# Down-weight differences in attention, kept split halves, and a rearranged block end in a decoder step on one core

## The chip, the cores and the metric

The kernel runs on one core of a Trainium2 chip. The metric is the device time of one execution in microseconds (us), as the median of several runs. Profiles are of one profiled execution.

The engines are named as in the profile: PE (TensorE, matmuls), PEld (its weight loads), DVE (VectorE), ACT (ScalarE), POOL (GpSimd) and SP (SyncE, which here only issues DMA transfers).

## The reference

One layer of a decoder is computed for 2048 prompt rows and for 8 × 4 sample rows that have a cache of 2048 keys and values. `h` stands for the rows of either group.

```python
q, k, v, u, g = split(rmsnorm(x, norm1_g) @ w_in)          # 1024 -> 5 x 512
att  = merge of 3 dilated-window attention branches (8 heads of 64)
gate = per chunk of 128 rows: tril(sgu_w) @ layernorm(g) + sgu_b
x = x + concat([att, u * gate]) @ w_out                    # 1024 -> 1024
h = rmsnorm(x, norm2_g)
x = x + (silu(h @ w_gate) * (h @ w_up)) @ w_down           # 1024 -> 2816 -> 1024
y = rmsnorm(x, final_g)
```

The outputs are `y` of both groups, the new keys and values, and the normalised `g` rows of the samples. The new caches of the samples are the old ones shifted by four rows, so 64 MB go from DRAM to DRAM.

## The kernel before

**Stages.** The times are those of the trace. The kernel first computes the projections, the spatial gate and the samples' attention (0 to 560 us). Then comes prompt attention (560 to about 900 us). The output projection and the feed-forward part (FFN) follow in three blocks of 6, 6 and 4 row tiles. The last block also holds the sample rows. The output projection and norm of block 0 end at 985 us. FFN block 0 runs to 1480, a block end to 1600, FFN block 1 to 2040, a block end to 2160, FFN block 2 to 2520, and the closing norm to 2557 us.

**Split products.** Each fp32 product is made of three matmuls: high × high, high × low and low × high. An operand is split by an ACT copy that rounds to the high half, and a subtraction on DVE or POOL that leaves the low half. `split_dw` does this for down weights (lines 1644 and 1645).

**The FFN.** The hidden width is cut into NF = 22 slices `f`. The up part of a slice is seven products, `product(B, u, q)` with q from 0 to 6, of a seven-product scheme in place of eight. Its operands are sums of weight parts that POOL and ACT prepare for later slices (lines 1579 and 1583). Two slices together make one group n (0 to 10) of seven down products, `down_product(B, k)`, k = 7n + p. Their left operands are sums of the hidden parts, made by `h_even` after the even slice and `h_odd` after the odd one; `high_of` and `lows_of` split them. Their right operands are w_down parts or differences of those. A down product issues nine matmuls for six tiles (line 1660) and three accumulations on DVE (line 1662).

**Down weights.** During the projections `down_rows` loads two row groups of w_down, `down_sums` makes four differences on POOL, and `down_keep` stores all seven parts in the DRAM buffer `dd_d`. In every block, `load_dw` fetches part k into one of two ring places after the product k − 2 was issued, and `split_dw` splits it two up products ahead of its use. POOL takes all low halves in block 1 and those of even k in blocks 0 and 2; DVE takes the others.

**What sets the order.** Each engine works through its instructions in the order in which they were issued. Through the projections and attention, a hand-made table sets that order: `at(step, phase, fn, ...)` puts a call at a step and a phase within it, and all is issued in that order. Attention begins at step B0 = 240. In the FFN the order is that of the loops: `one(u, q)` issues an up product and what belongs beside it, and `later(n, fn)` puts a call n ticks ahead, where each up product or down product at a block end is a tick. SP is a single in-order queue for nearly all transfers. `roll(n)` issues n pieces of 512 KB of the cache copies on it.

**The block end.** `next_block` is called after the last up product of a block. It issues the previous block's last eight down products with `h_odd` and the splits of `w_out` in between. After them `open_unit` starts the output projection of each tile of the next block (24 matmuls, lines 1407 to 1409), whose left operand `split_cat` has split (line 1399, the low half on DVE). `first_end`, `second_unit` and the norm follow.

## Time and profile before

| what | value |
|---|---|
| median of the runs (3 runs: 2557.12 to 2560.17 us) | 2557.52 us |
| the profiled execution's own time | 2560.03 us |
| its span, first to last instruction | 2557.5 us |
| mean granted TensorE clock | 0.980 |
| matrix work: PE busy | 2421.8 us, 95% of the span |
| instructions | 40544 |
| data moved by DMA | 512.36 MB, mean 200 GB/s |

The share of busy time is an average over stages that differ. So the windows of the stages, with the idle time of PE in each, tell more than the totals do. A row of the waits gives the engine, the tile and line that waited, what ended the wait, and then the total in us, the number of times and the longest. A row of the timeline gives start, length, engine, line and operation, output and input tiles with their shapes, and in brackets the engine's idle time ahead of it with what ended it. In a group the two numbers behind the bar are the busy time in us and the mean ns of one instruction.

### The profile page before, as it was taken

What the parts mean: (1) busy time and instruction counts of PE and PEld (TensorE: products, weight loads), DVE (VectorE), ACT (ScalarE), POOL (GpSimd) and SP (SyncE); (2) the same over time, 40 slices, a digit from 0 to 9 for tenths busy, and PEclk for the clock granted to TensorE, in tenths of its full rate; (3) what the DMA queues carried; (4) which work ended last, traced back from release to release, by engine and by line L of the source; (5) the groups of instructions that cost most, each with busy time, mean ns of one, the idle gap of its engine ahead of it and who ended that gap; (6) DMA issues with size and microseconds to landing.
All of it is one profiled execution on the core that took longest, in us unless ns stands there. A gap on an engine that the chain in (4) does not pass through costs nothing. (4 is left out here: it accounts for less than half of the span.)

```text
span 2557.5 us, 40544 instructions
## 1 busy us (share of the span) xinstructions
PE 2421.8 (95%) x13764; PEld 2080.4 (81%) x13764; DVE 1710.7 (67%) x3302; ACT 1242.6 (49%) x2773; POOL 1441.3 (56%) x1152
## 2 busy tenths in 40 slices
PE   8998998999999998999999989999999989999997
PEld 7876776657888778888988978999999967888886
DVE  4557564214777645778778786677767776888876
ACT  6323333224766646655655446443434346444444
POOL 2117463103777746777777734666666644666665
PEclk9999998999999999999999999999999999999999
DMA  9976877895456463655656562766665554666663
GB/s 290 281 235 226 273 239 237 281 297 201 146 183 197 108 199 110 200 185 181 192 176 205 173 189 98 233 202 199 199 202 192 189 184 134 212 204 216 217 214 113
DMA packets 326722, 512.36 MB, mean 200 GB/s; under 512 B 32535, under 2 KB 164808, under 8 KB 321396
## 3 DMA queue, kind: packets, MB, share of 16 engines
q1 hardware_dynamic: 319668, 497.72, 60.8%
q10 hardware_dynamic: 6848, 12.06, 1.7%
q8 instruction: 109, 1.79, 0.3%
q14 instruction: 97, 0.79, 0.1%
HBM read 401.77 MB, written 178.03 MB: 227 GB/s over the span
## 5 line engine op out<-in xcount | busy, mean ns | idle before, releaser
L1583 POOL TENSOR_TENSOR op<-fr,op 128x512 fp32r<-128x512 f32 x385 | 511.6, 1342 | 221.3 <-ACT op L1579 116.8
L1750 PE MATMUL ps_m<-xh,op 128*128 128x384 f32 (+3 forms) x1904 | 607.1, 319 | 1.9 <-DVE zn L1771 1.7
L1752 PE MATMUL ps_m<-xh,op 128*128 128x384 f32 (+3 forms) x1904 | 606.1, 318 | 0.0
L1751 PE MATMUL ps_m<-xl,op 128*128 128x384 f32 (+3 forms) x1904 | 605.7, 318 | 0.1
L1660 PE MATMUL ps_o<-hop 128*128 128x512 f32 x1260 | 343.4, 403 | 37.3 <-POOL hop L1645 26.5
L1750 PEld LDWEIGHTS ps_m<-xh,op 128*128 128x128 f32 x1904 | 361.5, 190 | 14.0 <-issue 1.9
L1751 PEld LDWEIGHTS ps_m<-xl,op 128*128 128x128 f32 x1904 | 361.0, 190 | 9.7 <-DVE xl L1496 0.4
L1752 PEld LDWEIGHTS ps_m<-xh,op 128*128 128x128 f32 x1904 | 360.8, 189 | 0.0
L1662 DVE TENSOR_TENSOR acc<-acc,ps_o 128x512 f32<-128x512 f32 x448 | 295.2, 682 | 26.9 <-PE ps_o L1660 20.6
L1660 PEld LDWEIGHTS ps_o<-hop 128*128 128x128 f32 x1260 | 230.6, 189 | 90.4 <-POOL hop L1645 38.7
L1645 POOL TENSOR_TENSOR hop<-hop 128x512 fp32r<-128x512 f32 x140 | 186.5, 1332 | 173.9 <-ACT hop L1644 158.6
L1579 ACT ACTIVATE op<-fr 128x512 fp32r<-128x512 f32 x396 | 238.7, 620 | 3.1 <-PE ps_m L1752 2.1
L1790 ACT ACTIVATE ps_t<-zn 128x384 f32<-128x384 f32 (+1 forms) x126 | 58.5, 464 | 365.4 <-DVE zn L1773 191.4
L320 PE MATMUL ps_s<-wh,xh 128*128 128x512 f32 x480 | 199.1, 415 | 6.3 <-ACT xh L137 5.9
L322 PE MATMUL ps_s<-wh,xl 128*128 128x512 f32 x480 | 190.8, 397 | 0.0
L321 PE MATMUL ps_s<-wl,xh 128*128 128x512 f32 x480 | 190.7, 397 | 0.0
L1644 ACT ACTIVATE hop<-hop 128x512 fp32r<-128x512 f32 x210 | 130.9, 623 | 56.6 <-DMA hop<-dd_d 54.7
L538 POOL TENSOR_TENSOR pr<-kv,qb 96x512 f32<-96x512 f32 x32 | 46.1, 1441 | 162.3 <-DMA kv<-in_cache_k_dram 75.6
L320 PEld LDWEIGHTS ps_s<-wh,xh 128*128 128x128 f32 x480 | 92.0, 192 | 49.2 <-issue 23.7
L1660 PE MATMUL ps_m<-hop 128*128 128x512 f32 x420 | 121.2, 397 | 0.0
L1583 POOL TENSOR_TENSOR op<-pair,op 128x512 fp32r<-128x512 f32 x63 | 86.9, 1382 | 50.9 <-ACT op L1579 50.8
L322 PEld LDWEIGHTS ps_s<-wh,xl 128*128 128x128 f32 x480 | 92.0, 192 | 20.8 <-DVE xl L140 0.2
(514 smaller groups left out, 5064.0 us busy)
## 6 DMA issues: line engine op xcount, KB each, us to landing
fr<-ab_d SPq DMA_DIRECT2D x308, 256.0 KB
hop<-dd_d SPq DMA_DIRECT2D x210, 256.0 KB
out_ks_dram<-in_cache_k_dram SPq DMA_DIRECT2D x56, 512.0 KB
out_vs_dram<-in_cache_v_dram SPq DMA_DIRECT2D x56, 512.0 KB
ab_d<-fr SPq DMA_DIRECT2D x88, 256.0 KB
qk_d<-pair SPq DMA_DIRECT2D x64, 256.0 KB
ab_d<-pair SPq DMA_DIRECT2D x63, 256.0 KB
kv<-in_cache_k_dram SPq DMA_DIRECT2D x64, 192.0 KB
```

The source lines that it names most:

```text
L320: pe.matmul(o[j], xh[:, k, :], wh, start=(k == 0), stop=False)
L321: pe.matmul(o[j], xh[:, k, :], wl, start=False, stop=False)
L322: pe.matmul(o[j], xl[:, k, :], wh, start=False, stop=(k == KD - 1))
L1579: act.activation(ops[f, j][0], ab[f][j], AF.Copy)
L1583: (pool if f or j in POOL_LOW else dve).tensor_sub(lo_, ab[f][j], hi.bitcast(F32))
L1644: act.activation(hi, lo_.bitcast(F32), AF.Copy)
L1645: (dve if k % 2 and (B.last or B.b0 == 0) else pool).tensor_sub(lo_, lo_.bitcast(F32), hi.bitcast(F32))
L1660: pe.matmul(ps, l_, r_, start=(new and y == 0), stop=(y == 2), skip_group_check=True)
L1662: dve.tensor_add(x[:, cs], x[:, cs], ps)
L1750: pe.matmul(out, wh[:, ks], xh[:, :, k], start=(k == 0), stop=False)
L1751: pe.matmul(out, wh[:, ks], xl[:, :, k], start=False, stop=False)
L1752: pe.matmul(out, wl[:, ks], xh[:, :, k], start=False, stop=(k == 3))
```

## The change

The change has five parts.

1. `down_rows`, `down_sums` and `down_keep` move from the projections to attention (steps 243 + 14n and on). Of the four differences of a group, two are made on POOL and two on DVE. The three parts that are plain pieces of w_down are copied from DRAM to DRAM during the projections (`down_plain`).
2. Block 1 stores both halves of each split down weight of groups 0 to 9 in a new DRAM buffer, `ds_d` (`keep_dw`). Block 2 loads both halves from there and splits nothing. In block 0 DVE makes all low halves; in block 1 POOL does, as before.
3. In blocks 0 and 2 the subtraction and low halves of `h_even` are made on POOL.
4. `roll` is called twice per slice in every block, where it was once, three times and twice.
5. At a block end the last down products stand in another order, with two `open_unit` calls among them. Six splits of `w_out` come ahead of the block end. The weights of the last group are loaded into free places of the operand buffers, which are allocated once for all blocks. `h_last` does in four parts what `h_odd` did in three. `split_cat` is spread over later ticks, and makes the low halves of all but the first two tiles on POOL.

The order of instructions in the program changes at three places, which are shown as engine, line, operation, output and input tiles. The line numbers of the two kernels differ by 1 to 16. The first place is POOL's order in the projections, beside a group's differences (`tu`, `tw`), the layer norm (`zn`) and the samples' scores (`pr`), before:

```order
L632 TENSOR_TENSOR tu<-tw 128x512
L629 TENSOR_TENSOR tw<-tw 128x512
L385 TENSOR_TENSOR zn<-zn,lnb 128x512
L632 TENSOR_TENSOR tu<-tw 128x512
L632 TENSOR_TENSOR tu<-tw,tu 128x512
L538 TENSOR_TENSOR pr<-kv,qb 96x512
L538 TENSOR_TENSOR pr<-kn,qb 128x512
```

and now, in the same stage:

```order
L386 TENSOR_TENSOR zn<-zn,lnb 128x512
L141 TENSOR_TENSOR vnl<-zn,vnh 128x512
L386 TENSOR_TENSOR zn<-zn,lnb 128x512
L539 TENSOR_TENSOR pr<-kv,qb 96x512
L539 TENSOR_TENSOR pr<-kn,qb 128x512
```

The differences are gone from between the layer-norm additions; nothing else changed places. The second place is DVE's order at the end of block 0, from the accumulations of one down product (`acc`) to the low half of the first tile to be opened (`xl`, 128x1024), before:

```order
L1662 TENSOR_TENSOR acc_9639<-acc_9639,ps_m_15162 128x512
L1682 TENSOR_TENSOR hop<-ps_t_14976,hop 128x3x64
L1682 TENSOR_TENSOR hop<-ps_t_15057,hop 128x3x64
L1682 TENSOR_TENSOR hop<-zn,hop 128x384
L1682 TENSOR_TENSOR hop<-raw,hop 128x384
L1662 TENSOR_TENSOR acc_9289<-acc_9289,ps_o_15152 128x512
L1662 TENSOR_TENSOR acc_9543<-acc_9543,ps_o_15157 128x512
L1662 TENSOR_TENSOR acc_9639<-acc_9639,ps_m_15162 128x512
L1399 TENSOR_TENSOR xl_15105<-xl_15105,xh_15104 128x1024
```

and now, from the low half that the product ahead of it needs:

```order
L1698 TENSOR_TENSOR hop<-zn,hop 128x384
L1698 TENSOR_TENSOR hop<-ps_t_15099,hop 128x3x64
L1698 TENSOR_TENSOR hop<-ps_t_15017,hop 128x3x64
L1774 TENSOR_TENSOR raw<-ps_t_15099,zn 128x3x64
L1774 TENSOR_TENSOR raw<-ps_t_15017,zn 128x3x64
L1656 TENSOR_TENSOR xl_9303<-xl_9303,xh_9302 128x512
L1678 TENSOR_TENSOR acc_9312<-acc_9312,ps_o_15222 128x512
L1678 TENSOR_TENSOR acc_9566<-acc_9566,ps_o_15227 128x512
L1678 TENSOR_TENSOR acc_9662<-acc_9662,ps_m_15232 128x512
L1406 TENSOR_TENSOR xl_9303<-xl_9303,xh_9302 128x1024
```

The tile's low half (line 1399 before, 1406 now) came ahead of the last down products' accumulations and does so still; what PE does next after three down products is now that tile's opening. The third place is SP's order in block 2, with the loads of down weights (`hop`), of prepared weight parts (`fr`) and a piece of the cache copies, before:

```order
L1291 DMA out_vs_dram<-in_cache_v_dram 16x8192
L1640 DMA hop<-dd_d 128x512
L1538 DMA fr<-ab_d 128x512 x2
L1291 DMA out_vs_dram<-in_cache_v_dram 16x8064
L1640 DMA hop<-dd_d 128x512
L1538 DMA fr<-ab_d 128x512 x2
```

and now:

```order
L1301 DMA out_vs_dram<-in_cache_v_dram 16x8192
L1545 DMA fr<-ab_d 128x512
L1649 DMA hop<-ds_d 128x512 x2
L1545 DMA fr<-ab_d 128x512 x2
L1301 DMA out_vs_dram<-in_cache_v_dram 16x8192
```

A weight now takes two loads of 256 KB, out of `ds_d`, at the place where one out of `dd_d` stood.

```diff
+    ds_d = dram.tile([NF // 2, 7, 2, P, 512], F32, name="ds_d")
...
-    def down_rows(n):
-        for z in range(2):
-            dn[n, z] = w_ = sp.tile([P, 2, DA], F32, name="tw", tag="tw", bufs=2)
-            f = 2 * n + z
-            sync.dma_start(w_, A["w_down"][f * P:(f + 1) * P, :].rearrange("p (a c) -> p a c", a=2))
-    def down_sums(n, j):
-        (b11, b12), (b21, b22) = ((dn[n, z][:, 0], dn[n, z][:, 1]) for z in range(2))
-        if j == 1:
-            pool.tensor_sub(b12, b12, b11)
-            return
-        dn[n, "t", j] = t_ = sp.tile([P, DA], F32, name="tu", tag="tu", bufs=3)
-        pool.tensor_sub(t_, *((b22, b12) if j == 3 else (b22, b12) if j == 2 else (b21, dn[n, "t", 2])))
-    def down_keep(n, j):
-        if j < 2:
-            sync.dma_start(dd_d[n, :, 2 * j:2 * j + 2], dn.pop((n, j)))
-        else:
-            sync.dma_start(dd_d[n, :, j + 2], dn.pop((n, "t", j)))
+    def down_plain(n, j):
+        f, half = 2 * n + (j > 0), int(j == 3)
+        sync.dma_start(dd_d[n, :, j], A["w_down"][f * P:(f + 1) * P, half * 512:(half + 1) * 512])
...
-    for n, s0 in enumerate([80, 89, 98] + [134 + 10 * i for i in range(NF // 2 - 3)]):
-        at(s0, "misc", down_rows, n)
-        for j, x in ((3, 3), (1, 3), (2, 4), (4, 4)):
-            at(s0 + x, "out", down_sums, n, j)
-        for j, x in ((3, 5), (0, 5), (2, 6), (4, 6), (1, 6)):
-            at(s0 + x, "store", down_keep, n, j)
+    for n in range(NF // 2):
+        for y, j in enumerate((0, 2, 3)):
+            at(134 + 6 * n + 2 * y, "store", down_plain, n, j)
...
+    def down_rows(n):
+        for z in range(2):
+            dn[n, z] = w_ = ap_.tile([P, 2, DA], F32, name="tw", tag="tw", bufs=4)
+            f = 2 * n + z
+            sync.dma_start(w_, A["w_down"][f * P:(f + 1) * P, :].rearrange("p (a c) -> p a c", a=2))
+    def down_sums(n, j, eng):
+        (b11, b12), (b21, b22) = ((dn[n, z][:, 0], dn[n, z][:, 1]) for z in range(2))
+        if j == 1:
+            eng.tensor_sub(b12, b12, b11)
+            return
+        dn[n, "t", j] = t_ = ap_.tile([P, DA], F32, name="tu", tag="tu", bufs=6)
+        eng.tensor_sub(t_, *((b22, b12) if j < 4 else (b21, dn[n, "t", 2])))
+    def down_keep(n, j):
+        if j == 1:
+            sync.dma_start(dd_d[n, :, 1], dn.pop((n, 0))[:, 1])
+        else:
+            sync.dma_start(dd_d[n, :, j + 2], dn.pop((n, "t", j)))
+    for n in range(NF // 2):
+        s0 = B0 + 3 + 14 * n
+        at(s0, "misc", down_rows, n)
+        for j, x, eng in ((3, 5, pool), (1, 6, dve), (2, 7, pool), (4, 8, dve)):
+            at(s0 + x, "store", down_sums, n, j, eng)
+        for j, x in ((3, 8), (1, 9), (2, 10), (4, 11)):
+            at(s0 + x, "store", down_keep, n, j)
...
+    def split_cat(B, i, eng=dve):
         ch, cl, a, b = B.late.pop(i)
         act.activation(ch[:, a:b], cl[:, a:b].bitcast(F32), AF.Copy)
-        dve.tensor_sub(cl[:, a:b], cl[:, a:b].bitcast(F32), ch[:, a:b].bitcast(F32))
+        eng.tensor_sub(cl[:, a:b], cl[:, a:b].bitcast(F32), ch[:, a:b].bitcast(F32))
...
-        sync.dma_start(x[1].bitcast(F32), dd_d[n, :, PLACE[p]])
+        if B.last:
+            for z in range(2):
+                sync.dma_start(x[z].bitcast(F32), ds_d[n, p, z])
+        else:
+            sync.dma_start(x[1].bitcast(F32), dd_d[n, :, PLACE[p]])
     def split_dw(B, k):
         hi, lo_ = B.dw[k]
         act.activation(hi, lo_.bitcast(F32), AF.Copy)
-        (dve if k % 2 and (B.last or B.b0 == 0) else pool).tensor_sub(lo_, lo_.bitcast(F32), hi.bitcast(F32))
+        (pool if B.b0 else dve).tensor_sub(lo_, lo_.bitcast(F32), hi.bitcast(F32))
+    def keep_dw(B, k):
+        n, p = divmod(k, 7)
+        for z in range(2):
+            sync.dma_start(ds_d[n, p, z], B.dw[k][z].bitcast(F32))
...
+        eng = pool if B.last or B.b0 == 0 else dve
         if plain:
             s3 = a21
         else:
             s3 = op_view(zn_tile()[:, 0:(b - a) * P], 0, b - a)
-            dve.tensor_sub(s3, a11, a21)
+            eng.tensor_sub(s3, a11, a21)
         high_of(B, 2, s3, a, b)
-        lows_of(B, 0, a11, a, b)
-        lows_of(B, 2, s3, a, b)
+        lows_of(B, 0, a11, a, b, None, eng)
+        lows_of(B, 2, s3, a, b, None, eng)
...
+    def h_last(B, u, part):
+        n = B.nt // 2
+        a12, a22 = ([u["raw"][z].rearrange("p (j o w) -> p o j w", o=2, w=B.w)[:, o, :, 0:64] for z in range(2)] for o in range(2))
+        a11, a21 = (B.h0[:, o, :, :, 0:64] for o in range(2))
+        if part == 0:
+            for z in (1, 0):
+                high_of(B, 4, a12[z], 0, n, z)
+            for z in (1, 0):
+                lows_of(B, 4, a12[z], 0, n, z)
+        elif part == 1:
+            u["s1"] = op_view(zn_tile()[:, 0:n * P], 0, n)
+            u["s2"] = op_view(zn_tile()[:, 0:n * P], 0, n)
+            for z in (1, 0):
+                dve.tensor_add(u["s1"][:, :, z], a21[:, :, z], a22[z])
+            dve.tensor_sub(u["s2"], u["s1"], a11)
+            high_of(B, 1, u["s2"], 0, n)
+            for z in (1, 0):
+                high_of(B, 3, a22[z], 0, n, z)
+        elif part == 2:
+            lows_of(B, 1, u["s2"], 0, n)
+            u["s4"] = op_view(raw_tile()[:, 0:n * P], 0, n)
+            for z in (1, 0):
+                lows_of(B, 3, a22[z], 0, n, z)
+            for z in (1, 0):
+                dve.tensor_sub(u["s4"][:, :, z], a12[z], u["s2"][:, :, z])
+            high_of(B, 5, u["s1"], 0, n)
+            high_of(B, 6, u["s4"], 0, n)
+        else:
             lows_of(B, 5, u["s1"], 0, n)
             lows_of(B, 6, u["s4"], 0, n)
...
-            later(3 + 2 * (j + skip), split_cat, B, i)
+            later((3, 7, 11, 13, 15, 17)[j + skip], split_cat, B, i, dve if j < 2 else pool)
         half1_load(*range(4))
         later(3, half1_load, *range(4, KD))
+        for s in (6, 7):
+            later(s - 5, split_wo, B, 0, s, lambda s: op_tile())
         for y, fn in enumerate(finals):
-            later(9 + y, fn)
+            later(13 + y, fn)
         for y, i in enumerate(order):
-            later(16 + 2 * y, first_end, B, i)
+            later(8 + 2 * n + 2 * y, first_end, B, i)
         for y in range(4):
-            later(10 + 3 * y, half1_split, B, 2 * y, 2 * y + 1)
-            later(12 + 3 * y, sources, B, 0, *((2 * y, 2 * y + 1) if y < 3 else (6,)))
-        K = 7 * (NF // 2 - 1)
-        for y in range(-1, 7):
-            if 0 <= y + 1 < 3:
-                h_odd(prev, prev.u, y + 1)
-            if y == -1:
-                split_dw(prev, K + 6)
-            down_product(prev, K + y)
-            split_wo(B, 0, y + 1, lambda s: op_tile())
-            tick()
-        for i in order:
+            later(13 + 2 * y, half1_split, B, 2 * y, 2 * y + 1)
+            later(15 + 2 * y, sources, B, 0, *((2 * y, 2 * y + 1) if y < 3 else (6,)))
+        K, opens = 7 * (NF // 2 - 1), list(order)
+        def downs(*ks):
+            for k in ks:
+                down_product(prev, k)
+                tick()
+        h_last(prev, prev.u, 0)
+        downs(K - 1)
+        split_dw(prev, K + 2)
+        h_last(prev, prev.u, 1)
+        downs(K + 4)
+        h_last(prev, prev.u, 2)
+        split_dw(prev, K + 3)
+        downs(K)
+        h_last(prev, prev.u, 3)
+        split_dw(prev, K + 5)
+        open_unit(B, opens.pop(0))
+        split_dw(prev, K + 6)
+        downs(K + 1, K + 2)
+        open_unit(B, opens.pop(0))
+        downs(K + 3, K + 5, K + 6)
+        for i in opens:
...
-                    load_dw(B, 7 * (f // 2) + q, op_tile())
                     if q > 0:
-                        split_dw(B, 7 * (f // 2) + q - 1)
-            if f + 1 < NF and q in (1, 3, 5)[:(1, 3, 2)[bi]]:
+                        split_wo(nb, 0, q - 1, lambda s: op_tile())
+                    for y, p in {3: ((0, 0), (1, 1)), 4: ((2, 2), (3, 3)), 5: ((4, 5), (5, 6))}.get(q, ()):
+                        c0 = (y - 4) * 28 * 64 + 512 if y > 3 and nb.last else y * 28 * 64
+                        load_dw(B, 7 * (f // 2) + p, tuple(x[:, c0:c0 + 512] for x in pool_["X"]))
+                    for p in {5: (0,), 6: (4, 1)}.get(q, ()):
+                        split_dw(B, 7 * (f // 2) + p)
+            if f + 1 < NF and q in (1, 4):
...
+                    if x == t_ and p == 5 and n + 2 == NF // 2 and nb:
+                        down_product(B, k)
+                        load_dw(B, k + 6, B.ring[k % 2])
+                        continue
                     if n < 0 or n + 1 == NF // 2:
                         continue
-                    if x == t_ - 2:
+                    if x == t_ - 2 and not B.last:
                         split_dw(B, k)
+                    if x == t_ - 1 and nb and nb.last:
+                        keep_dw(B, k)
```

22 lines of the change are left out of this document (10 added, 12 removed).

## Prediction

> **What bounds the kernel now.** I read the totals first, then one window per stage, then what TensorE (PE) waited for, and last the timeline around the longest of those waits. The totals:
>
> ```profile
> span 2557.5 us, 40544 instructions
> PE 2421.8 (95%) x13764; PEld 2080.4 (81%) x13764; DVE 1710.7 (67%) x3302; ACT 1242.6 (49%) x2773; POOL 1441.3 (56%) x1152
> ```
>
> PE is the bound: all that is not PE work is 2557.5 − 2421.8 = 135.7 us, and the change leaves the number of matmuls as it is. So nothing in it can give more than those idle times, plus what a lowered TensorE clock costs. Where they lie is told by the windows (columns: length, busy time of each engine, granted clock, DMA share, GB/s): the later part of the projections, attention, feed-forward (FFN) block 0, the end of block 0, block 1, its end, block 2.
>
> ```profile
> core 0: us, PE busy (x) PEld busy (x) DVE busy (x) ACT busy (x) POOL busy (x), PEclk, DMA share, GB/s
> 185.00:420.00 235.00, 206.38 (x937) 163.20 (x937) 150.79 (x293) 83.65 (x140) 144.95 (x103) 0.94 0.76 245
> 560.00:985.00 425.00, 406.65 (x3134) 329.61 (x3132) 254.20 (x637) 260.71 (x649) 247.60 (x258) 0.97 0.55 169
> 985.00:1480.00 495.00, 477.73 (x2540) 444.53 (x2541) 381.44 (x612) 282.58 (x712) 363.41 (x272) 0.99 0.59 184
> 1480.00:1600.00 120.00, 111.26 (x586) 93.83 (x585) 85.59 (x191) 67.16 (x138) 51.33 (x38) 0.99 0.46 145
> 1600.00:2040.00 440.00, 440.00 (x2326) 413.24 (x2325) 313.22 (x537) 176.61 (x366) 274.87 (x212) 1.00 0.63 201
> 2040.00:2160.00 120.00, 104.97 (x498) 85.10 (x497) 82.02 (x183) 63.04 (x133) 51.72 (x40) 0.93 0.47 148
> 2160.00:2520.00 360.00, 339.26 (x2174) 303.58 (x2174) 293.12 (x579) 169.45 (x401) 233.27 (x176) 0.99 0.65 210
> ```
>
> PE is idle for 28.6 us in the projection window, 17.3 in block 0, 20.7 in block 2, 8.7 and 15.0 at the two block ends, and not at all in block 1. The clock took (1 − 0.94) × 235 = 14 us more in the projections and 8 us at the second block end. The waits of PE in the whole run (total, times, longest):
>
> ```profile
> PE ps_o L1660 <- POOL hop L1645: 26.5, 30, 3.2
> PE ps_t L414 <- ACT vnh L137: 12.7, 2, 9.8
> PE ps_o L1660 <- DVE acc L1662: 12.6, 9, 2.2
> PE ps_t L414 <- DVE un L422: 7.9, 3, 4.0
> PE ps_o L320 <- DVE zn L381: 3.7, 1, 3.7
> ```
>
> The largest is the down product (L1660) that waits for the second half of a weight split (L1645) on POOL. The same view for blocks 0 (first row) and 2 alone:
>
> ```profile
> PE ps_o L1660 <- POOL hop L1645: 16.0, 14, 3.2
> ...
> PE ps_o L1660 <- POOL hop L1645: 10.5, 16, 0.9
> PE ps_o L1660 <- ACT hop L1644: 6.1, 8, 1.0
> PE ps_o L1660 <- DVE hop L1645: 3.9, 4, 1.0
> ```
>
> So the splits of down weights explain nearly all the idle time of block 0 (16.0 of 17.3) and of block 2 (20.5 of 20.7).
>
> **The change part by part.** Durations of the operations that it moves (groups: busy, mean ns):
>
> ```profile
> L632 POOL TENSOR_TENSOR tu<-tw 128x512 f32<-128x512 f32 x22 | 29.5, 1342 | 84.0 <-DMA raw<-in_w_in_dram 27.8 <-DMA tw<-in_w_down_dram 26.9 <-DMA qk_d<-pair 25.1
> L1645 POOL TENSOR_TENSOR hop<-hop 128x512 fp32r<-128x512 f32 x140 | 186.5, 1332 | 173.9 <-ACT hop L1644 158.6 <-ACT hs L1806 11.0 <-PE ps_m L1752 3.6
> L1645 DVE TENSOR_TENSOR hop<-hop 128x512 fp32r<-128x512 f32 x70 | 73.3, 1048 | 17.0 <-ACT hop L1644 15.8
> L1644 ACT ACTIVATE hop<-hop 128x512 fp32r<-128x512 f32 x210 | 130.9, 623 | 56.6 <-DMA hop<-dd_d 54.7 <-POOL op L1583 1.9
> L1662 DVE TENSOR_TENSOR acc<-acc,ps_o 128x512 f32<-128x512 f32 x448 | 295.2, 682 | 26.9 <-PE ps_o L1660 20.6
> L1682 DVE TENSOR_TENSOR hop<-ps_t,hop 128x192 fp32r<-128x192 f32 x88 | 28.7, 346 | 0.0
> L1399 DVE TENSOR_TENSOR xl<-xl,xh 128x1024 fp32r<-128x1024 f32 x11 | 15.6, 1416 | 14.2 <-ACT xh L1398 14.1
> ```
>
> 1. The weight differences leave the projections: 44 POOL subtractions, 44 × 1.34 = 59 us of POOL time. What they cost there is seen at the longest PE wait:
>
> ```profile
> 375.08 1.48 POOL L629 TENSOR_TENSOR tw<-tw 128x512 f32<-128x512 f32 x1
> ...
> 377.77 1.28 POOL L632 TENSOR_TENSOR tu<-tw 128x512 f32<-128x512 f32 x1
> 379.13 1.29 POOL L632 TENSOR_TENSOR tu<-tw,tu 128x512 f32<-128x512 f32 x1
> 380.37 1.26 POOL L385 TENSOR_TENSOR zn<-zn,lnb 128x512 f32<-128x512 f32 x1
> 381.67 0.63 ACT L137 ACTIVATE vnh<-zn 128x512 fp32r<-128x512 f32 x1 [6.30 <-POOL zn L385]
> 390.22 0.58 PE L414 MATMUL ps_t<-vnh,wg_h 128*128 128x256 f32 x1 [9.82 <-ACT vnh L137]
> ```
>
> Three differences stand ahead of a layer-norm addition (L385) on POOL, and ACT waits 6.30 us for it; behind ACT's conversion stands the rest of the chain that PE needs. Without them the addition starts up to 1.48 + 1.28 + 1.29 = 4.05 us sooner, 41% of the 9.82 us. The same 41% of this and its kin (12.7 + 7.9 + 3.7 = 24.3) is 10 us; with a little of the 14 us of clock I take −12. Ends: −2 (the chain itself keeps PE waiting), −22 (nearly all the wait goes). In place of loads, sums and stores SP gets 33 copies within DRAM; the DMA share there, 0.76, has room for a copy that no engine awaits.
>
> 2. The differences in attention: 22 on POOL, 22 on DVE, plus 22 loads and 44 stores on SP. POOL is busy 248 of 425 us and DVE 254. What idle time there is, and whom they wait for:
>
> ```profile
> DVE pt L927 <- PE ps_t L916: 42.6, 47, 1.6
> ...
> POOL e L980 <- DVE st L975: 73.2, 26, 11.3
> ```
>
> POOL waits 73.2/26 = 2.8 us a time, so a difference of 1.34 us fits. DVE waits 42.6/47 = 0.9 us a time, so one of 1.05 us shows 0.15 us, 22 × 0.15 = 3.3 us; with the DMA beside it I take +4. Ends: 0 (all hidden), +52 (22 × 1.34 + 22 × 1.05, all exposed). The low end is the nearer, since attention's engines are each idle 40% of the time.
>
> A rule of the Trainium skill speaks against this part and against item 4: "SBUF — State Buffer", section "Who interferes with whom", says that a GpSimd operation and a DVE operation with both inputs in SBUF take turns on a shared port, the other one standing still for the whole instruction. The trace agrees as far as it goes: a DVE split, both inputs in SBUF, takes 1048 ns, an accumulation of the same size from PSUM 682. By the rule alone the upper end of item 2 would hold and the sum below be −37 − 4 + 52 = +11; by the slack that the rows show it stays at −37.
>
> 3. Block 0: the 35 splits that POOL did go to DVE. PE's 16.0 us wait is for POOL's. On DVE a split takes 1.05 us instead of 1.33 and stands behind accumulations of 0.68, not behind POOL's weight sums of the next slices (1.34 each). DVE has 495 − 381 = 114 us free, gets 35 × 1.05 = 37 and gives up item 4's. I take 13 of 16.0 as gone; ends −20 (all 17.3 us idle and half of the (1 − 0.99) × 495 = 5 us of clock) and −3 (DVE queues them as POOL did).
>
> 4. h_even's subtraction and lows on POOL in blocks 0 and 2: about 3 per feature slice, for one slice in two: 11 × 3 = 33 operations, at 1.33 us 44 us on POOL, which gives up 35 × 1.33 = 47 of splits in block 0 and in block 2. They feed down products several units of PE work later; POOL, with 131 and 127 us free there, covers them: nothing.
>
> 5. Block 1 writes both halves of 70 weights to DRAM (140 stores, 256 KB): 35 MB in 440 us, at 201 GB/s moved now with a DMA share of 0.63. PE has no idle time there to lose or gain, so only a load that comes late costs: +1, ends 0 and +12. The rolls (DRAM copies, two a slice in every block) move the same bytes.
>
> 6. Block 2 loads both halves and splits nothing: −70 ACT copies (0.62), −35 DVE and −35 POOL subtractions. All three waits above fall away, 20.5 us. Instead PE waits for the DMA itself:
>
> ```profile
> 2212.96 0.37 SPq L1640 DMA_DIRECT2D hop<-dd_d  x1
> 2216.06 0.63 ACT L1644 ACTIVATE hop<-hop 128x512 fp32r<-128x512 f32 x1 [0.39 <-DMA hop<-dd_d]
> ```
>
> Issue to use is 3.1 us. Copy and subtraction of 0.62 + 1.33 us fall out of that path and a second transfer of 256 KB comes in behind the first, about equal. I leave 2.5 us for late ones: −18; ends −8 and −23 (with clock).
>
> 7. The block ends. The windows around the last eight down products of block 0 and of block 1, and the first PE row of those of block 0 with the first one after them:
>
> ```profile
> 1477.40:1505.10 27.70, 21.18 (x86) 16.02 (x85) 25.40 (x43) 10.81 (x20) 11.71 (x9) 0.94 0.54 156
> 2049.50:2074.95 25.45, 19.41 (x75) 14.30 (x74) 21.63 (x37) 9.06 (x17) 12.20 (x10) 0.93 0.51 145
> ...
> 1479.52 1.55 PE L1660 MATMUL ps_o<-hop 128*128 128x512 f32 x6
> 1505.08 0.39 PE L1407 MATMUL ps_t<-op,xh 128*128 128x512 f32 x1
> ```
>
> DVE, busy 25.4 of 27.7 us, is the bound here; PE is idle 6.5 us. Six matmuls take 1.55 us, a product of nine 2.3, eight 18.6. Afterwards only three stand ahead of the first opened tile: 7.0 us. DVE's list to the low half of that tile: 9 accumulations × 0.682 = 6.1, four splits × 1.05 = 4.2, eight small operations of 0.35 = 2.8, two of hidden rows about 1.5, the tile's low 1.4: 16.0. PE would wait 9 us instead of 6.5, and perhaps 1 before the second opening: +4 (ends −8, all hidden behind 24 matmuls per opening; +10). At the end of block 1 the splits are on POOL and the sample rows, which need no low half, open first: 16.0 − 4.2 − 1.4 = 10.4 against 7.0, a wait of 3.4 instead of 25.45 − 19.41 = 6.0: −3 (ends −9, +3).
>
> The sum: −12 + 4 − 13 + 4 + 1 − 3 − 18 = −37 us against the profiled execution's own 2560.0: 2523. The median of the runs is 2557.5, 2.5 us lower, which puts the forecast at 2521.
>
> **The rivals.** A, the forecast: 2521, its own range 2508 to 2536.
>
> B, the weave hides DVE's list at both block ends (−8 and −9 instead of +4 and −3) and the projections give 4 more and block 0 another 3. For it: an opening brings PE work that needs little from DVE. Against: DVE's list leads to that very opening. 2521 − 12 − 6 − 4 − 3 = 2496 to, with half of these, 2508; say 2503.
>
> C, the freed waits don't come: the layer-norm chain itself keeps PE waiting in the projections (−4), DVE queues the splits of block 0 (−8), block 2's loads land late (−10), attention costs +8, the block ends +2 and block 1 +1. Together −11: 2546. For it: block 2 loads 70 × 256 KB = 18 MB more in 360 us, with DMA at 0.65, and DVE is its busiest engine after PE in block 0.
>
> D, slower: the attention differences sit on in-order queues in chains where PE follows within a microsecond (DVE waits 0.9 us a time for PE, so PE soon waits for DVE). All exposed it is +52, and 2557.5 − 41 + 52 = 2569; it decides from 46 us exposed on with the other terms as forecast (−41), and from 24 beside C's (−19). Against it: POOL's slack of 2.8 us.
>
> E, slower: in block 1 a place of the two-place ring is free again only when its stores have left. Load 3.1, copy 0.62, split 1.33, stores of about 3.1: 8.2 us. A place comes round every four of the block's 154 up products, 4 × 440/154 = 11.4 us. At landings of 5.6 us the cycle is 13.2, PE waits 1.8 us for each of 35 rounds, and 2557.5 − 38 + 61 is 2581; it decides from landings of 5.3 us on (1.2 × 35 = 43). Against it: the 3.1 us.
>
> **How the numbers follow.** A 0.52, B 0.20, C 0.17, D 0.05, E 0.02, no change to speak of (C with 8 us more, some 2555) 0.04. The measurement tells no change from one of under 0.2%, 5.1 us. Faster: A, B and C, 0.89, less 0.01 for C's upper edge; same: that and the 0.04; slower: D and E. The range runs from 2498, within B, to 2550, beyond C; it leaves out D, E, the no-change case and the outer edge of B.
>
> **What would show it.** Right: the wait of L1660 for weight splits gone from blocks 0 and 2, with PE idle under 6 us in each; the projection window at some 16 us less idle time or clock loss; attention longer by under 8 us; at the end of block 0 a wait of PE for the opened tile's low half of about 9 us. Wrong: PE waiting for DMA in block 2 or 1, PE waits for pt or e in attention, or the L414 waits unchanged.

## The result and the profile after

The changed kernel takes 2578.14 us (median of 4 runs, 2574.83 to 2581.95) against 2557.32 for the kernel before: 1.0081 times as long, 95% interval 1.0061 to 1.0100. It is slower, by 21 us. The forecast was 2521. The totals of the changed kernel's profiled execution (its own time is 2574.83 us):

```profile
span 2573.1 us, 40785 instructions
PE 2428.4 (94%) x13764; PEld 2083.0 (81%) x13764; DVE 1683.4 (65%) x3254; ACT 1206.2 (47%) x2703; POOL 1388.9 (54%) x1130
```

DVE, ACT and POOL each do less, and yet PE's idle time is larger. Fixed times of day no longer compare two kernels whose stages are shifted, so both are cut at the same events: the first and last score matmul of attention, and the first and last up product of each FFN block. The windows of the changed kernel, cut so (the projections, attention, output projection of block 0, block 0, its end, block 1, its end, block 2):

```profile
core 0: us, PE busy (x) PEld busy (x) DVE busy (x) ACT busy (x) POOL busy (x), PEclk, DMA share, GB/s
0.00:570.83 570.83, 547.50 (x2554) 414.34 (x2555) 272.35 (x512) 209.69 (x344) 147.78 (x109) 0.99 0.74 231
570.83:900.16 329.33, 294.45 (x2548) 243.39 (x2547) 228.67 (x544) 202.75 (x517) 232.53 (x236) 0.94 0.68 217
900.16:991.93 91.77, 82.60 (x403) 65.70 (x403) 44.13 (x101) 53.21 (x119) 40.71 (x37) 0.96 0.54 167
991.93:1484.32 492.39, 481.13 (x2560) 446.69 (x2560) 358.35 (x616) 285.49 (x720) 356.76 (x277) 0.99 0.65 207
1484.32:1587.38 103.06, 91.15 (x405) 73.21 (x404) 77.51 (x157) 52.10 (x108) 42.07 (x25) 0.97 0.47 152
1587.38:2082.59 495.21, 481.22 (x2560) 443.57 (x2559) 349.00 (x586) 194.43 (x402) 296.60 (x228) 1.00 0.73 236
2082.59:2185.34 102.75, 80.82 (x341) 61.93 (x340) 66.59 (x153) 50.10 (x109) 44.05 (x30) 0.91 0.43 140
2185.34:2544.24 358.90, 354.05 (x2337) 322.78 (x2338) 270.79 (x543) 143.29 (x356) 216.03 (x184) 1.00 0.80 272
```

And the kernel before, cut at the same events, for attention and block 1:

```profile
596.21:885.80 289.59, 281.81 (x2548) 233.50 (x2547) 204.23 (x522) 199.42 (x517) 199.66 (x215) 0.98 0.54 166
1575.49:2049.22 473.73, 471.80 (x2561) 443.96 (x2559) 335.71 (x586) 193.30 (x401) 294.52 (x228) 1.00 0.61 195
```

Attention, with the same 2548 matmuls, takes 40 us longer: PE's idle time there grows from 7.8 to 34.9 us, and the other 12.6 us are longer matmuls, at a granted clock of 0.94 instead of 0.98. Block 1, which had hardly any idle time (1.9 us), takes 21 us longer. All stages, from the cuts (us):

| stage | before | after | difference | forecast |
|---|---|---|---|---|
| projections | 596.2 | 570.8 | −25.4 | −12 |
| attention | 289.6 | 329.3 | +39.7 | +4 |
| output projection, block 0 | 94.4 | 91.8 | −2.6 | 0 |
| block 0 | 499.0 | 492.4 | −6.6 | −13 |
| end of block 0 | 96.3 | 103.1 | +6.7 | +4 |
| block 1 | 473.7 | 495.2 | +21.5 | +1 |
| end of block 1 | 95.3 | 102.7 | +7.4 | −3 |
| block 2 | 384.2 | 358.9 | −25.3 | −18 |
| closing | 28.8 | 28.8 | 0 | 0 |

They add up to +15.5, the difference of the two spans (2573.1 − 2557.5). What PE waits for in attention (first two rows), block 1 (third) and at the end of block 1:

```profile
PE ps_s L946 <- DVE st L873: 16.5, 7, 6.3
PE ps_s L867 <- DVE st L873: 15.1, 13, 4.0
...
PE ps_o L1676 <- POOL hop L1656: 10.6, 16, 0.9
...
PE ps_t L1480 <- ACT xns L1467: 5.3, 1, 5.3
PE ps_o L1419 <- ACT wol L138: 4.8, 1, 4.8
```

**Attention.** PE waits for DVE's row minima (st, line 873), and DVE itself waits for POOL's differences. The view of DVE's waits in attention, and then one such place, on POOL, DVE and PE:

```profile
DVE tw L1231 <- POOL tu L1234: 15.7, 6, 5.1
...
DVE tu L1234 <- POOL tu L1234: 10.5, 4, 3.8
```

```profile
729.78 1.26 POOL L1234 TENSOR_TENSOR tu<-tw 128x512 f32<-128x512 f32 x1 [4.82 <-DMA tw<-in_w_down_dram]
...
731.08 1.51 DVE L1231 TENSOR_TENSOR tw<-tw 128x512 f32<-128x512 f32 x1 [4.07 <-POOL tu L1234]
732.51 0.41 DVE L905 COPY pt<-ps_t 128x256 f32<-128x256 f32 x1
732.85 0.81 DVE L873 CUSTOM_DVE_ANT_0 e<-ps_s,b 128x640 f32<-128x640 f32 x1
...
733.81 0.55 PE L867 MATMUL ps_s<-k,qh 128*128 128x256 f32 x1 [3.97 <-DVE st L873]
```

The difference on DVE overwrites `b12`, which POOL's difference of one step before still has to read. POOL is late here, because the rows are (4.82 us); DVE's queue stands for 4.07 us, with copies and scores of attention behind, and PE then waits 3.97 us. POOL waits for rows only twice in the stage. At the next place (738.27, where DVE stands for 3.80 us) it is late because its subtraction and the strided operands of attention (lines 958 and 938) stand ahead of the difference in its own queue.

**Block 1.** SP's, ACT's waits there, and one round on SP, ACT, POOL and PE:

```profile
SPq L1651 <- DMA ds_d<-hop: 224.8, 69, 5.5
...
ACT hop L1655 <- DMA hop<-dd_d: 129.9, 40, 6.8
```

```profile
1915.11 0.86 SPq L1661 DMA_DIRECT2D ds_d<-hop  x2
...
1919.68 0.33 SPq L1651 DMA_DIRECT2D hop<-dd_d  x1
...
1924.51 0.63 ACT L1655 ACTIVATE hop<-hop 128x512 fp32r<-128x512 f32 x1 [5.51 <-DMA hop<-dd_d]
...
1925.22 1.27 POOL L1656 TENSOR_TENSOR hop<-hop 128x512 fp32r<-128x512 f32 x1 [3.81 <-ACT hop L1655]
...
1926.55 0.73 PE L1676 MATMUL ps_o<-hop 128*128 128x512 f32 x2 [0.84 <-POOL hop L1656]
```

The next load may not overwrite a half before its store has landed: stores at 1915.11, load at 1919.68, data 4.8 us later, split, and PE waits 0.84 us. The whole loss lies at the down products: added up over the block, the time from one matmul's start to the next is 20.9 us longer than before inside the down products, and only 0.5 us longer between the up products' matmuls. The profile counts 12.1 us of it as idle time of PE (14.0 instead of 1.9) and the rest as busy time (481.2 instead of 471.8); why the matmuls beside a wait are booked as longer isn't shown.

### The profile page after: what moved, and what is told of

It is laid out like the page before. It is cut to its first block, busy times and chain, and to the rows that moved or that the text cites. A ratio compares the mean times of both kernels' runs of the same rounds, so it can differ in the third digit from the quotient of the medians.

```text
span 2573.1 us, 40785 instructions
## 1 busy us (share of the span) xinstructions
PE 2428.4 (94%) x13764; PEld 2083.0 (81%) x13764; DVE 1683.4 (65%) x3254; ACT 1206.2 (47%) x2703; POOL 1388.9 (54%) x1130
## 4 chain that ended last, share of the span: by engine, by line
PE 36%; POOL 13%; issue 11%; DVE 8%; DMA 7%; ACT 5%; SPq 1%; POOLq 0%; DVEq 0%; ACTq 0%
POOL op L1590 5%; PE ps_o L1676 5%; PE ps_m L1799 4%; PE ps_m L1801 4%; PE ps_m L1800 4%; DMA hop<-dd_d 2%; PE ps_m L1676 2%; PE ps_s L867 1%; POOL sq L938 1%; ACT fr L1558 1%; ACT op L1586 1%; PE ps_o L922 1%; DMA ds_d<-hop 1%; DVE acc L1678 1%; PE ps_s L321 1%
## 5 line engine op out<-in xcount | busy, mean ns | idle before, releaser
L1590 POOL TENSOR_TENSOR op<-fr,op 128x512 fp32r<-128x512 f32 x385 | 505.9, 1330 | 252.4 <-ACT op L1586 240.7
L1656 POOL TENSOR_TENSOR hop<-hop 128x512 fp32r<-128x512 f32 x71 | 91.8, 1293 | 168.9 <-ACT hop L1655 156.3
L1655 ACT ACTIVATE hop<-hop 128x512 fp32r<-128x512 f32 x142 | 88.8, 625 | 178.5 <-DMA hop<-dd_d 131.3
L1590 POOL TENSOR_TENSOR op<-pair,op 128x512 fp32r<-128x512 f32 x63 | 92.6, 1470 | 61.2 <-ACT op L1586 58.1
L1656 DVE TENSOR_TENSOR hop<-hop 128x512 fp32r<-128x512 f32 x71 | 74.3, 1047 | 76.7 <-ACT hop L1655 71.7
```

Of the source, the lines that this page charges most:

```text
L1590: (pool if f or j in POOL_LOW else dve).tensor_sub(lo_, ab[f][j], hi.bitcast(F32))
L1655: act.activation(hi, lo_.bitcast(F32), AF.Copy)
L1656: (pool if B.b0 else dve).tensor_sub(lo_, lo_.bitcast(F32), hi.bitcast(F32))
```

## The experiments

Blocks 0, 1 and 2 repeat from run to run within 3 us where no edit touches them, the block ends within 3, the projections at 568 to 574 and attention at 329 to 335 us (PE's idle time there is 34 to 37 us in all of these, and the clock 0.92 to 0.94). So edits in different stages could go into one kernel. The last three kernels start from v1_mended, the others from the changed kernel. In m2_early, m3_nosum and p1_dveonly a part of the arithmetic is left out, as said there: they serve to measure and are no replacement. The table gives stage lengths of one profile each (us), cut as above, and the median time of the runs.

| kernel | attention | block 0 | its end | block 1 | its end | block 2 | time |
|---|---|---|---|---|---|---|---|
| before | 289.6 | 499.0 | 96.3 | 473.7 | 95.3 | 384.2 | 2557.3 |
| after | 329.3 | 492.4 | 103.1 | 495.2 | 102.7 | 358.9 | 2578.1 |
| a1_lag | 310.0 | 492.5 | 103.1 | 495.7 | 102.6 | 358.1 | 2561.3 |
| a2_pool | 333.1 | 492.5 | 103.4 | 496.5 | 104.4 | 358.4 | 2581.2 |
| k1_nokeep | 333.4 | 492.5 | 103.3 | 473.7 | 101.2 | 397.3 | 2594.1 |
| k2_keep0 | 331.6 | 538.3 | 106.0 | 473.4 | 104.9 | 358.1 | 2605.5 |
| m1_oldend | 335.2 | 492.5 | 99.2 | 476.1 | 95.6 | 358.6 | 2546.7 |
| m2_early | 309.8 | 492.5 | 111.6 | 474.4 | 97.5 | 356.7 | 2534.1 |
| m3_nosum | 287.8 | 482.5 | 104.0 | 494.2 | 103.4 | 357.6 | 2523.5 |
| m4_split0 | 332.0 | 508.8 | 100.4 | 496.1 | 102.3 | 356.5 | 2592.1 |
| v1_mended | 314.0 | 482.7 | 98.3 | 498.1 | 97.8 | 357.6 | 2544.9 |
| v2_halves | 297.6 | 482.4 | 99.1 | 502.9 | 97.5 | 358.7 | 2541.1 |
| p1_dveonly | 291.5 | 483.0 | 98.1 | 498.8 | 97.4 | 356.3 | 2523.7 |
| v4_alldve | 297.9 | 482.7 | 98.4 | 475.1 | 96.7 | 357.2 | 2507.9 |

**a1_lag: the differences further apart.**

```diff
-for j, x, eng in ((3, 5, pool), (1, 6, dve), (2, 7, pool), (4, 8, dve)):
+for j, x, eng in ((3, 5, pool), (1, 8, dve), (2, 10, pool), (4, 13, dve)):
```

> Edit: the attention differences keep their engines, and only stand further apart in the table: POOL at 5, DVE at 8, POOL at 10, DVE at 13 steps behind the load, instead of 5, 6, 7, 8. Theory W (wait): a DVE difference stands one step behind the POOL difference that it depends on, POOL is late, and DVE's in-order queue stands still with the attention scores behind it (DVE waited 26 us for tu in ten places). Then nearly all of the loss goes: attention from 329 us to about 300, the time to about 2550. Theory O (occupancy): the 22 operations on DVE, and two SBUF inputs beside a busy POOL, cost what they cost. The same instructions run, so attention stays within 5 us of 329 and the time within 5 us of 2578.

Attention went to 310.0 us, half of the way: the close spacing, with DVE standing for POOL, costs 19.3 us of the 39.7 (11.4 less idle time of PE, the rest shorter matmuls as the clock went from 0.94 to 0.98). Since attention also measured up to 335 us without an edit, the 19.3 is good to some 6 us. Some 20 us stay that both theories had not placed.

**a2_pool: all four on POOL** (`dve` becomes `pool` in the same line).

> Edit: all four differences of a group on POOL at the same steps, none on DVE. Theory W: DVE waits for nothing new, POOL has room for 44 x 1.3 us, attention about 298 us, the time about 2548, like the run with larger spacing or a little better. Theory O: DVE is relieved of 22 x 1.35 = 30 us, but POOL, which DVE and ACT wait for, gets 29 us more: attention 310 to 320, the time 2560 to 2570, while the run with larger spacing shows nothing.

Attention took 333.1 us, as much as before this edit. Both theories missed. DVE no longer waits for a difference, but the loss stays the same: attention follows POOL in other ways too. PE's waits there, in this run, and one place on DVE, POOL and PE:

```profile
PE ps_s L946 <- DVE st L873: 8.9, 5, 3.5
PE ps_o L970 <- ACT e L961: 7.3, 3, 4.3
PE ps_s L946 <- POOL sq L938: 4.9, 7, 1.1
```

```profile
779.77 3.10 DVE L1032 TENSOR_TENSOR dd<-f,s 128x16 f32<-128x16 f32 x1
782.79 0.16 DVE L1033 TENSOR_TENSOR dd<-f,st 128x16 f32<-128x16 f32 x1
...
781.48 1.35 POOL L1234 TENSOR_TENSOR tu<-tw 128x512 f32<-128x512 f32 x1
...
786.45 0.52 PE L946 MATMUL ps_s<-sq 128*128 128x128 f32 x3 [3.51 <-DVE st L873]
```

ACT's exponentials (line 961) come behind POOL's subtraction (line 958), and POOL also makes the strided operands (line 938): the second and third rows are POOL's queue. The first row has another reason. Four of its waits, 8.7 us in all, follow small operations of DVE (lines 1032, 1033, 1034 and 1036) that read two operands in SBUF. Beside POOL's work they take up to 3.10 us, where one of the same size also takes 0.16, and the row minima stand behind them. Together these operations take 23.9 us in the stage, against 15.1 in the kernel before. So POOL's differences cost time in two ways: by POOL's queue, and by longer operations on DVE.

**k1_nokeep: nothing stored in block 1, block 2 splits as before.**

```diff
-                    if x == t_ - 1 and nb and nb.last:
-                        keep_dw(B, k)
-                    if x == t_ - 2 and not B.last:
+                    if x == t_ - 2:
```

> Edit: no halves are stored in block 1, and block 2 loads and splits its down weights as the kernel before did; all else as changed. Theory R (ring): in block 1 a load waits for the landing of its place's two stores (SP waited 224.8 us for 69 of them), so splits come late. Then block 1 goes from 495 to about 474 us, block 2 from 359 to about 384, and the time is about 2582. Rival S: block 1 is late for something else in the change (rolls, the last group's early loads, more work on POOL): block 1 stays near 495, block 2 goes to 384, the time to about 2603.

Block 1 came back to 473.7 us: the stores are the whole of its 21.5 us. Block 2 took 397.3 us, 13 more than before the change, with the splits of before and h_even on POOL; the latter is the likely reason, but wasn't run alone there.

**k2_keep0: the halves kept in block 0** (`keep_dw` where `B.b0 == 0`; blocks 1 and 2 load both halves).

> Edit: block 0 stores the halves instead of block 1, and blocks 1 and 2 load both halves (groups 0 to 9). Theory R: block 1 has no split and no store in its ring any more and goes from 495 to 474 or a little less. Block 0's ring gets the cycle of load, split, store: about 4.8 + 0.6 + 1.1 + 0.9 + 3.7 us and waits for order between them, some 12.8, against the 4 x 492/154 = 12.8 us that a place comes round in: 0 to +12 us there. The time is 2557 to 2569. Rival S: block 1 stays near 495 and the time at 2575 or more.

Block 1 reached 473.4 us, as the ring theory had it, though loads took the place of splits. But block 0 lost 45.9 us, almost four times the upper expectation. A ring place took 14.2 us a round there, not 12.8: from the stores to the next load 5.6, from the load to ACT's copy 4.6, the split 1.6, and 2.4 more until the stores. In the changed kernel's block 1 the load took 3.4 us; block 0 has a DMA share of 0.78 where that block has 0.73, but why its loads are later isn't shown.

**m1_oldend: the block ends of before; in block 1 the low half is stored first** (`for z in (1, 0)` in `keep_dw`).

> Two edits, in stages that are read apart. Block ends: the order of before is restored (eight down products, then all openings; weight loads and splits of the last group as before; norm chains of the last tiles at their old ticks). If the woven order costs what the stages show, the two ends go from 103 to 96 us and from 103 to 95; if they are longer because of the other parts (DVE's splits, later weights), they stay within 2 us of 103. Block 1: of each kept weight the low half is stored first. The next load goes into the low half's place, so by the ring theory it can start about 0.4 us sooner and block 1 goes from 495 to between 480 and 490 us; if the ring isn't the cause it stays at 495. Time by both theories: about 2553.

Both ends are shorter: 99.2 and 95.6. So the woven order costs 3.8 and 7.1 us, and 2.9 at the end of block 0 come from elsewhere. Block 1 fell by 19.1 us to 476.1, more than expected, with two stores exchanged; the ring theory holds (SP's wait for the stores fell from 224.8 to 157.1 us).

**m2_early: the finals (the closing norms and stores of the finished block's tiles) at tick 9, the stores at once behind the split, a wider lag** (`x == t_ - 2` for `keep_dw`; differences at 8, 11, 13, 16). In the woven order the last eight down products are issued at ticks 1 to 3, 6, 7 and 10 to 12, so finals from tick 9 on leave the last of them out of the output.

> Three edits, in stages that are read apart. End of block 1: the finals start at tick 9 again instead of 13. The sample rows' norm there waited 7.7 us for the store of an output tile whose buffer it takes; sooner stores give 103 to about 97 us; if that wait only moves, it stays at 103. Block 1: a weight's halves are stored at once behind its split, one up product (2.9 us) sooner. Ring theory: the stores have landed when the place is free, block 1 at 474 to 478 us. Rival: SP now stands for the split with the loads behind it and block 1 stays above 488. Attention: differences at 8, 11, 13, 16 steps behind the load. If late rows are part of what the first spacing (310 us) left, attention goes to about 300; if the rest is the operations' own time, it stays at 308 to 312. Time by the first theories: 2530 to 2535.

Block 1 took 474.4 us, a second sign of the ring. The second block end went to 97.5, by 5.2 us, near the 5.3 that PE waited. The first got 8.5 us longer; PE waits 3.8 us there for low halves that POOL makes of opened tiles, and the rest wasn't followed up. Attention stayed at 309.8: late rows are not what a1_lag left. At the end of block 1 the changed kernel had shown what the finals' store holds up, the sample rows' norm that takes the buffer:

```profile
ACT xns L1459 <- DMA out_yp_dram<-acc: 7.7, 1, 7.7
```

**m3_nosum: no arithmetic in attention; h_even on DVE.**

> Two edits, in stages that are read apart. Attention: the rows are loaded and as many bytes are stored, but no difference is computed (the stored parts are plain rows). If operations and their waits cause the 40 us, attention goes to 290 to 293 us; if the transfers cause what the first spacing left, it stays near 308. h_even's subtraction and lows on DVE again in blocks 0 and 2: if POOL has room for them, as forecast, block 0 and block 2 stay within 2 us of 492 and 359; if they held up ACT (its highs waited 55 us in block 0 for POOL's s3), block 0 falls by 3 us or more; if DVE is what PE follows, both get longer by 3 us or more.

Attention took 287.8 us: making the differences causes all the 40 us there, not the transfers (the stage behind it took 100.1 instead of 91.8, so 8 us come back there). Block 0 fell to 482.5, by 9.9 us, half of it idle time of PE and half shorter matmuls. ACT's waits in block 0, in the changed kernel and here:

```profile
ACT hop L1702 <- POOL zn L1715: 54.8, 12, 7.4
```

```profile
ACT hop L1702 <- DVE zn L1715: 4.7, 7, 0.7
```

ACT's copy of the high half (line 1702) waits for POOL's subtraction (line 1715), and the down weights' copies stand behind it on ACT.

**m4_split0: in block 0 even low halves and the whole last group on POOL.**

> Edit: in block 0 the low halves of even weights, and of the whole last group, are made on POOL (before: even ones on POOL; changed: all on DVE). Theory: block 0's gain of 6.6 us is that PE no longer waits for POOL's splits, so block 0 goes from 492 to 499 or more, with h_even on POOL as well perhaps 505. At the end of block 0 DVE's list ahead of the first opened tile gets shorter by four splits, 4.2 us, and the end goes from 103 to about 99 us; if DVE's list isn't what PE waits for, it stays at 103. Time: 2580 to 2590.

Block 0 took 508.8 us, 16.4 more, which is also 9.8 more than before the change: about the price of `h_even` on POOL once again. PE waits 20.4 us for POOL's splits there:

```profile
PE ps_o L1676 <- POOL hop L1656: 20.4, 15, 2.3
```

The end of block 0 went to 100.4, by 2.7 us of the 4.2 that leave DVE's list.

**v1_mended: four mends together**: a1_lag, m1_oldend's two edits, h_even on DVE, and the stores at once behind the split.

> The change with four mends: differences 5, 8, 10, 13 steps behind the load; the block ends of before; h_even on DVE in all blocks; kept halves stored at once behind the split, the low one first. If stages add up, from the runs so far: projections 573, attention 310, output projection 94, block 0 482, end 99, block 1 474, end 96, block 2 358, closing 29: 2515 us of span, time about 2517, faster than the kernel before by 1.5%. If the mends disturb one another (block 0 gets back its waits with DVE fuller at the block end, or block 1 stands for its early stores), 2525 or more.

It is faster than before, 0.9951 (0.9936 to 0.9966), but 28 us slower than the sum of stages. Block 1 took 498.1 us, though each of its two mends alone had given 476 or 474. SP's waits show why, here and in m2_early, where the high half is stored first:

```profile
SPq L1664 <- POOL hop L1659: 231.2, 69, 5.9
```

```profile
SPq L1661 <- ACT hop L1655: 99.8, 62, 3.6
...
SPq L1661 <- POOL hop L1656: 66.0, 69, 1.3
```

With the low half first SP waits until POOL has made it, and issues both stores only then, ahead of the next load: SP's order closes a loop of its own, load, split, stores, next load. From one split on POOL to the next it then takes 6.63 us on average over the block (POOL's splits at 1899.13, 1905.75 and 1912.84, for instance). With the high half first its store is out while POOL works, and the average is 6.24 us, as in the kernel before.

**v2_halves: five groups of differences on POOL in the late projections, six in attention every 24 steps.**

> As the mended version, but groups 0 to 4 of the differences are made on POOL in the late projections (steps 164 to 210), the other six in attention every 24 steps. If attention's 20 us are paid per difference, 24 of 44 cost 11 there instead of 20, and the 20 late ones in the projections, where POOL is mostly idle from 420 us on, 3 to 8 us: 2509 to 2515. If the projections lose as they did before the change (25 us for 44), it is 2518.

It takes 2541.1 us, 0.9937 (0.9916 to 0.9958). Attention took 297.6 us, the projections 575.1 against 571.5 in v1_mended: as forecast by the first theory, with block 1's loss on top.

**p1_dveonly: as v1_mended, with POOL's differences left out.** The end of block 0 also has the last group's low halves on POOL.

> As the mended version, with two edits, in stages that are read apart. Attention: POOL's two differences of a group are left out (plain rows are stored in their place), DVE's two are made with no dependence on them. Whose time are the 20 us that the larger spacing left? If POOL's, attention is 288 to 293 us; if DVE's, 302 to 310; if both, about 298. End of block 0: with the old order there, the last group's low halves on POOL: if its 3 us over before come from DVE's splits, the end goes from 99 to 96.

Attention took 291.5 us: the 22 on DVE cost 2 us (4 against m3_nosum), the 22 on POOL the rest. The end of block 0 stayed at 98.1 us. PE's idle time in it is back at that of the kernel before (6.9 against 6.8 us; 8.3 in v1_mended), so the splits did cost some 1.4 us; what is left are longer matmuls, at a clock of 0.97 where it was 0.98.

**v4_alldve: as v1_mended, with all differences on DVE and further apart, and the high half stored first.**

```diff
+for j, x, eng in ((3, 8, dve), (1, 11, dve), (2, 13, dve), (4, 16, dve)):
```

> As the mended version, with two differences. Attention: all four differences of a group on DVE, at 8, 11, 13 and 16 steps behind the load, none on POOL. Theory P: what the spacing left there (20 us) is POOL's share, whose few microseconds stand ahead of the strided scores; DVE's 22 alone cost 2 us. Then 44 on DVE cost 4 to 10 us and attention is 294 to 300. Rival: DVE only looked cheap with 22, it is the engine that PE follows there: attention is 310 or more. Block 1: the halves are stored at once behind the split, but the high one first. If the mended version's block 1 (498 us) came from SP standing for POOL's low half with the next load behind it, it is 474 to 476 now; if from h_even or the old block end, it stays near 498. Time 2502 to 2512 if both hold, 2540 if neither.

It takes 2507.86 us (median of 5), 0.9819 (0.9802 to 0.9836) of the kernel before, and is faster than both kernels. The 44 differences cost 8.3 us in attention, block 1 took 475.1. Its totals:

```profile
span 2500.6 us, 40766 instructions
PE 2402.5 (96%) x13764; PEld 2070.2 (83%) x13764; DVE 1745.9 (70%) x3350; ACT 1208.0 (48%) x2703; POOL 1301.4 (52%) x1034
```

DVE is busier than in the changed kernel by 62 us, POOL less by 88, and the time is shorter by 70.

## Why the prediction was wrong

- **Item 2 (attention, +4, measured +39.7) is the step that failed first.** It added up the operations' own time against mean slack. It left out that the differences depend on one another across two engines, one step apart, so that DVE's queue stands for POOL's: 19.3 us by a1_lag. And POOL's mean wait of 2.8 us was taken for its room. With the larger spacing POOL's 22 still cost 18 to 22 us (310.0 and 314.0 against 291.5), although POOL has 40.1 us of such waits left there: a mean wait doesn't say whether there is room at the place where a difference falls. On DVE, where the rows gave 0.9 us of slack and 3.3 us for 22, it was right: 1.9 measured. Rival D was the right kind of loss with the wrong bound: it decides alone from 46 us, and 40 came.
- **Item 5 (block 1, +1, measured +21.5) failed too, and rival E was what happened.** Rival E's cycle of 8.2 us was load 3.1, copy and split 1.95, stores 3.1. Averaged over the block it measured 13.0: from the load to the copy 3.4, copy and split 2.1, from the first store to the next load 5.2, and a term that the sum didn't have, 2.3 from the end of the split to the stores, which were issued one up product later. In the round shown the place's next stores follow at 1928.18, a cycle of 13.1 us, where four up and two down products take PE about 12.4 us without the waits (m2_early). E was given 0.02 as if landings had to reach 5.3 us. D and E together are 61 us; the gains of the rest could have borne either alone.
- **Item 4 (h_even on POOL, nothing) cost 9.9 us in block 0** (m3_nosum). Its cover was named as POOL's free time; what counts is that ACT's copies of the high halves wait for POOL's subtraction, 54.8 us, with the weights' copies behind them.
- **Item 3 (block 0, −13) was right in itself:** with h_even back on DVE it is −16.5 (m3_nosum), some 11 of idle time, two thirds of what the block had, and 5 of shorter matmuls; item 4 took 9.9 of it back.
- **Item 6 (block 2, −18) was right in its mechanism, and too small:** −25.3. It lies beyond that item's end of −23: PE's idle time fell by 15.9 us, about as forecast, and the matmuls took 9.4 us less at a clock of 1.00 instead of 0.98, which the term had nearly left out. The splits' waits went; PE waits only 2.1 us for `hop<-ds_d`. By k1_nokeep the kept halves are worth 38 us beside h_even on POOL.
- **Item 1 (projections, −12) was right in direction, measured −25.4.** It lies beyond that item's end of −22: PE's idle time fell by 19.1 us, most of it at line 414 (now 415), and the matmuls took 6.3 us less as the clock rose (0.97 to 0.99 over the stage), which the term had nearly left out. No run separates POOL's order from the transfers that left the stage with it.
- **Item 7 (the block ends, +4 and −3): +6.7 and +7.4.** At the first, PE was to wait 9 us for the opened tile's low half; it waits 3.5 us for ACT's high half and 3.2 for DVE's low halves. DVE's list is a part of the reason: m4_split0, with four splits off it, took 2.7 us off. At the second the working stopped at the last down products; the finals that moved from tick 9 to 13 delayed an output tile's store, whose buffer the sample rows' norm takes, and PE waited 5.3 us.

The DVE and POOL rule of the Trainium skill ("SBUF — State Buffer", "Who interferes with whom"), which would have put item 2 at its upper end by blocking, doesn't explain the half of the loss that a1_lag took away: the same operations ran on the same engines there, and the 22 on DVE were lengthened even more (10.6 us above 22 × 0.68 in sum, 7.9 in the changed kernel). In single operations the trace agrees with the rule. In v4_alldve a DVE difference takes 0.68 to 0.69 us wherever POOL does nothing at the time; POOL is at work during all or most of each of the 15 that take 0.9 us or more, and the 44 take 11.2 us longer than 44 × 0.68. So blocking can be the whole of the 8.3 us that attention loses there. How the 18 to 22 us of POOL's 22 divide between blocking and POOL's queue wasn't separated by a run; a2_pool shows both.

## What to carry to other kernels

Work that is moved to a stage with idle engines must be priced by the queue that it stands in, and not by the busy share of the engine: which instruction behind it does the bound engine follow, and does the moved work itself wait for another engine? A chain of dependent operations that is split over two in-order queues at small distance makes each stand for the other; a larger distance took half of the loss away. On one queue the chain is cheap only if the bound engine doesn't follow that queue closely: the 44 differences cost 8.3 us on DVE and 43.5 on POOL, though DVE's stood further apart, and that wasn't tried on POOL. A buffer that is stored before it is loaded again needs the landing times of both, from rows of the busy stage, added to the whole cycle, and the order on the issuing queue counts as much as the buffer.

## What the runs showed that was not expected

Exchanging two stores of 256 KB (the low half first) gave 19.1 us, and so did issuing them one product sooner (20.8), but both together gave nothing (498.1 us): SP then stood 231.2 us for POOL, and v4_alldve, with the stores in the other order, took 475.1. And moving some 33 of DVE's operations to POOL cost block 0 9.9 us, while PE's own waits there named ACT and DVE, never POOL: the engine that made the others late does not stand in PE's rows.
